# High parts of q and k written straight into the scores' tiles, k's low part beside zeros, and new engine times in the planner

## The chip, the core and the metric

One core of a Trainium2 chip runs the whole program. The metric is device microseconds (us) of one execution. The kernel before took 2547.5 us (median of three runs, 2544.88 to 2548.47).

The names of the profile: PE is TensorE (matmuls; PEld its weight loads), DVE is VectorE, ACT is ScalarE, POOL is GpSimd, SP is SyncE, whose queue issues the DMA transfers. Each engine takes its instructions strictly in the order in which they were written for it, and waits at the first whose inputs or output buffer are not ready.

## The reference, cut to what matters

The program is a two-layer encoder on 512 tokens of 1024 features, in float32. Each layer is:

```
x = x + 0.5 * swiglu_ffn(x, ffn1_norm, w_gate, w_up, w_down)      # 1024 -> 2816 -> 1024
h = rms_norm(x, mix_norm)
aq, ak, av, bq, bk, bv, cq, ck, cv, cg, gates = split(h @ w_in)
y_a = diff_attention(rope(norm(aq)), rope(norm(ak)), av, ...)     # 4 heads x 2 score maps, v 128 wide, rms norm of each head
y_b = chunk_attention(norm(bq), norm(bk), bv, rel_bias)           # 8 heads, 64 wide
y_c = silu(cg) * rms(retention(rope(cq), rope(ck), cv))           # 4 heads, q and k 64 wide, v 128 wide
merged = sum over a, b, c of sigmoid(gate) * (y @ w_branch)
x = x + merged @ w_out
x = x + 0.5 * swiglu_ffn(x, ffn2_norm, ...)
```

In A and B the attention weights are `softmax(q·k * scale + mask or bias)`; in C they are `q·k * decay`. q and k have 64 features per head.

## The kernel before, in words

**Precision.** A float32 product is made of three matmuls: each operand is split into a high part in the `fp32r` type (one ACT copy) and a low part (what is left, one DVE subtraction), and the program multiplies hi·hi, hi·lo and lo·hi. For the scores, where q and k have only 64 features and TensorE contracts over 128 rows, the three products fit into two matmuls: q's tile holds hi in one half of its 128 rows and lo in the other; k's first tile holds hi in both halves, k's second tile holds lo in both halves (`scores`, `dots`).

**The main stream.** Weights come in 212 pieces of 128x1024 per layer as `wr` (one SP transfer of 512 KB each, L195), ACT writes `wh`, DVE `wl`, and 5088 matmuls of 128x512 per layer use them. These are called main matmuls below and counted from the start of a layer: ffn1 to 1584; the projections of A's q, k, v and B's q, k, v, 96 each, to 2160; **branch A**: its eight gate projections (`proj` of `xn`) to 2352, four projections for C's output gate (`c_gates`) to 2448, then 96 products of A's result with its branch weights to 2544; C's q, k and v to 2736; **branch B**: eight gate projections to 2928, products to 3024; **branch C**: gate projections to 3216, products to 3312; `w_out` to 3504; ffn2 to 5088. This order is fixed in `mixer` and `branch`.

**The side programs.** Everything else of the mixers is written as Python generators, and a planner mixes them into the main stream while the program is written. `prep` normalises q or k of A or B (`rsqrt` on 128x32 numbers, eleven or twelve small DVE operations, then one DVE operation for each of four tiles `z`), transposes them on PE in four head pairs (four transposes each), splits each bank of PSUM into `qh` and `ql`, and lets `stack` and `twice` copy the halves into the scores' tiles `qk` by SP transfers (L661). `c_prep` does the same for C, whose halves come rotated out of the projection, by transfers of 32 rows (L1012). `a_head`, `b_head` and `c_head` make scores, softmax, transposes of the weights and products with v. In A and C a head ends in `settle_head`: the result `yu` and its square `sq` are copied from PSUM, `yh` and `yl` are the split of the square, and two matmuls against `ones` total the square over features; the totals go into `ss`. `finish` then takes two heads at a time: `rsqrt_wide` on 128x512 numbers (v, r, then three rounds of three DVE operations, and for C one more), two small SP transfers `rh<-r` per head (L763), one or two DVE operations on `yu`, and its split into `yh` and `yl` for the branch products.

**The planner.** `Model` keeps an estimated time for each engine and adds an estimated cost to it for every instruction that is written (`note`, L89); `sent` (L85) estimates when a transfer has landed. After every main matmul `tick` (L249) may let one side program take one step, if the Model says that its inputs are ready, that no backlog is above 5 us, and that the pace allows it (`due`). `branch` (L1029) needs a finished list `ys`: where its flag is not up when its gate projections are written, it calls `drain(flag)` (L1042), and for branch C `drain()` (L1044) in any case: the side programs are then written out with no main matmul between them. All the Model's numbers act on the order alone; the chip never sees them.

**Buffers.** All 128x512 tiles come from one ring of 72 buffers (`big`), in the order in which they are asked for; eight PSUM banks likewise.

Of the kernel before, what the change touches and what calls it, by code (L numbers as in the profile page):

```python
# [51 lines left out]
class Model:  # L52
# [3 lines left out]
    def __init__(self):  # L56
        self.t = dict(pe=0.0, dve=0.0, act=0.0, pool=0.0)
        self.wrote = {}
        self.read = {}
        self.slots = [0.0] * 8  # L60
        self.owner = {}

# [21 lines left out]

    def sent(self, ap, wait=2500):  # L85

        self.wrote[self.key(ap)] = max(self.t.values()) + wait, "pe"

    def note(self, eng, op, named):  # L89
# [5 lines left out]
        if "dma" in op:  # L95
            for a in outs:
                self.wrote[self.key(a)] = max(self.t[eng], self.t["pe"]) + 2500, eng
            return
        if eng == "pe":
            if op == "transpose":  # L100
                d = 109
            elif named["rhs"].dtype == F32R:
                d = n / 2.37 if n >= 256 else 213
            else:
                d = max(n, 64) * 1.7
# [17 lines left out]
def then(*aps):  # L123

    return aps, False, 0
# [7 lines left out]
def room(*aps):  # L133

    return aps, True, Kernel.MARGIN


class Kernel:
# [467 lines left out]
    def prep(self, z, ms, out, flag, tabs=None, final=None, gain=None):  # L606
# [4 lines left out]
        for b in range(NB):  # L611
# [12 lines left out]
            yield then()  # L624
        parts = None
        for pr in range(4):
            yield room(*z)
            bank = self.bank()
            for b in range(NB):
                nc.tensor.transpose(bank[:, b * P:(b + 1) * P], z[b][:, pr * P:(pr + 1) * P], self.ident)  # L630
            if pr:
                self.stack(parts, out, flag)
            yield then(bank)
            hi, lo = parts = self.big(F32R, "qh"), self.big(F32R, "ql")
            g = 1.0 if gain is None else gain
            nc.scalar.activation(out=hi, in_=bank, func=AF.Copy, scale=g)
            yield then(hi)
# [4 lines left out]
            self.free(bank)  # L642
        yield then(lo)
        self.stack(parts, out, flag)
# [12 lines left out]
    def twice(self, a, b, own, other):  # L657

        t = self.big(F32R, "qk")
        for o, x in ((own, a), (other, b)):  # L660
            self.nc.sync.dma_start(out=t[o].bitcast(F32), in_=x.bitcast(F32))  # L661
        self.model.sent(t)
        return t

# [110 lines left out]
    def a_head(self, h, st):  # L775
# [11 lines left out]

        yield room(*(st[s][2 * h + c][0] for s in "qk" for c in range(2)))
        for i in range(NB + 1):
# [24 lines left out]
    def b_head(self, h, st):  # L814
        nc = self.nc
        tb = self.table()
        es = self.weights()
        yield room(*(st[s][h][0] for s in "qk"))
        for i in range(NB):
# [29 lines left out]
    def c_head(self, h, st):  # L849
# [3 lines left out]
        pt = self.turned()  # L853
        yield room(q[0], k[0], k[1])
        for j in range(NB):
# [141 lines left out]
    def c_prep(self, halves, out, s):  # L997


        parts = []  # L1000
        for y in halves:
            parts.append((yield from self.split_side(y)))
        yield then(parts[1][1])
        for h in range(4):
            hi, lo = ([p[i][32 * h:32 * h + 32] for p in parts] for i in range(2))
            a, b = h % 2 * 64, 64 - h % 2 * 64
            both = []
            for one, two in ((hi, hi), (lo, lo)) if s == "k" else ((hi, lo),):
                t = self.big(F32R, "qk")
                for at, pieces in ((a, one), (b, two)):  # L1010
                    for i, x in enumerate(pieces):
                        self.nc.sync.dma_start(out=t[at + 32 * i:at + 32 * i + 32].bitcast(F32), in_=x.bitcast(F32))  # L1012
                self.model.sent(t)
                both.append(t)
            out.append((both[0], both[-1]))
            self.flags.add(f"{s}C{h}")
# [196 lines left out]
```

## Time and profile before

| | |
|---|---|
| median of 3 runs | 2547.5 us (2544.88 to 2548.47) |
| the profiled execution's own time | 2552.16 us |
| its span | 2550.4 us |
| mean granted TensorE clock | 0.996 |
| PE busy | 2517.2 us (99%) |
| DVE, ACT, POOL busy | 1375.7 (54%), 919.8 (36%), 138.3 us (5%) |
| SP transfers into scores' tiles | 96 `qk<-qh`, 96 `qk<-ql`, 48 `qk<-yh`, 48 `qk<-yl` |

The span runs from the first instruction to the last; the execution's own time is 1.8 us longer. A layer's projections and branches lie between about 380 and 850 us in the first layer and between about 1650 and 2120 us in the second. All compute instructions have line L48 (they pass through the planner's wrapper), so they are told apart by their tiles: `bank<-xh,wh` is a projection, `bank<-ident,z` a transpose in `prep`, `bank<-yh,ones` a total, `bank<-ident,e` a transpose of softmax weights `e`.

### The profile page before, as it was taken

To read this page: it belongs to the slowest core of one execution; us is meant where nothing else is said; L and a number is where in the kernel's file an instruction comes from. 1 tells how busy PE (TensorE), PEld (TensorE's weight loads), DVE (VectorE), ACT (ScalarE), POOL (GpSimd) and SP (SyncE) were. 2 spreads that over 40 slices of the span, in tenths; PEclk is the share of its full clock that TensorE was granted. 3 is DMA by queue.
4 is the path that set the end of the run, shared out by engine and by line. 5 is a ranking of instruction groups with operands and counts; after the bars stand their busy time and mean duration, and the time that the engine had idled before them with its cause. 6 is when DMAs were issued, how large, how long until landed. Compare 5 with 4: busy or idle time off the path is not lost.

```text
span 2550.4 us, 28931 instructions
## 1 busy us (share of the span) xinstructions
PE 2517.2 (99%) x11226; PEld 2054.4 (81%) x11226; DVE 1375.7 (54%) x2180; ACT 919.8 (36%) x1397; POOL 138.3 (5%) x104
## 2 busy tenths in 40 slices
PE   9999999999999999999999999999999999999999
PEld 7888887887878888888888888878878788888887
DVE  6334338776758653433353433477767576543332
ACT  4333224553443433332233332245534433333321
POOL 0000101000102100000000001010001021000000
PEclk9999999999999999999999999999999999999999
DMA  5333344527433433333333333344274324333332
GB/s 167 92 99 91 118 130 123 134 83 190 115 105 83 140 99 99 92 99 94 96 92 98 91 97 114 120 133 123 85 196 113 106 76 146 99 94 99 91 111 71
DMA packets 96617, 280.91 MB, mean 110 GB/s; under 512 B 13536, under 2 KB 14944, under 8 KB 96480
## 3 DMA queue, kind: packets, MB, share of 16 engines
q1 hardware_dynamic: 95760, 278.45, 38.2%
q8 instruction: 88, 1.44, 0.2%
q10 hardware_dynamic: 720, 0.62, 0.1%
q14 instruction: 49, 0.40, 0.0%
HBM read 237.08 MB, written 6.29 MB: 95 GB/s over the span
## 4 chain that ended last, share of the span: by engine, by line
PE 93%; DVE 3%; SPq 2%; DMA 1%; issue 0%; ACT 0%; DVEq 0%
PE bank L48 93%; SPq L661 1%; SPq L1012 1%; DVE wl L48 1%; DMA qk<-ql 1%; DVE e L48 0%; DMA x<-in_xt 0%; DVE n L48 0%; DVE g L48 0%; DVE z L48 0%; DVE pt L48 0%; DVE r L48 0%; DMA qk<-yh 0%; DVE ql L48 0%; ACT wh L48 0%
## 5 line engine op out<-in xcount | busy, mean ns | idle before, releaser
L48 DVE TENSOR_TENSOR wl<-wr,wh 128x1024 fp32r<-128x1024 f32 x422 | 530.8, 1259 | 705.7 <-ACT wh L48 703.6
L48 PE MATMUL bank<-xh,wh 128*128 128x512 f32 x1920 | 758.8, 395 | 0.0
L48 PE MATMUL bank<-xl,wh 128*128 128x512 f32 x1920 | 757.6, 395 | 0.1
L48 PE MATMUL bank<-xh,wl 128*128 128x512 f32 x1920 | 756.3, 394 | 0.0
L48 ACT ACTIVATE wh<-wr 128x1024 fp32r<-128x1024 f32 x422 | 445.4, 1056 | 775.2 <-PE bank L48 671.2
L48 PEld LDWEIGHTS bank<-xh,wh 128*128 128x128 f32 x1920 | 361.9, 188 | 78.2 <-ACT xh L48 1.2
L48 PEld LDWEIGHTS bank<-xl,wh 128*128 128x128 f32 x1920 | 362.0, 189 | 77.9 <-DVE xl L48 1.7
L48 PEld LDWEIGHTS bank<-xh,wl 128*128 128x128 f32 x1920 | 361.9, 188 | 77.7
L48 PE MATMUL bank<-ph,wh 128*128 128x512 f32 x704 | 276.6, 393 | 0.0
L48 PE MATMUL bank<-pl,wh 128*128 128x512 f32 x704 | 276.6, 393 | 0.0
L48 PE MATMUL bank<-ph,wl 128*128 128x512 f32 x704 | 276.6, 393 | 0.0
L48 PE MATMUL bank<-wl,xh 128*128 128x512 f32 x448 | 179.2, 400 | 0.0
L48 PE MATMUL bank<-wh,xh 128*128 128x512 f32 x448 | 178.8, 399 | 0.0
L48 PE MATMUL bank<-wh,xl 128*128 128x512 f32 x448 | 178.2, 398 | 0.0
L48 PEld LDWEIGHTS bank<-ph,wh 128*128 128x128 f32 x704 | 132.4, 188 | 29.6
L48 PEld LDWEIGHTS bank<-ph,wl 128*128 128x128 f32 x704 | 132.4, 188 | 29.4
L48 PEld LDWEIGHTS bank<-pl,wh 128*128 128x128 f32 x704 | 132.4, 188 | 29.4
L48 ACT ACTIVATE e<-e,m 128x128 f32<-128x128 f32 (+3 forms) x128 | 71.4, 558 | 118.8 <-DVE m L48 105.0
L48 ACT ACTIVATE t<-t 128x512 f32<-128x512 f32 x88 | 55.6, 632 | 162.5 <-DVE t L48 162.5
L48 POOL TENSOR_TENSOR acc<-acc,sq 128x512 f32<-128x512 f32 x30 | 39.4, 1314 | 1112.1 <-PE bank L48 567.7
L48 PEld LDWEIGHTS bank<-wh,xh 128*128 128x128 f32 x448 | 84.3, 188 | 17.0
L48 PEld LDWEIGHTS bank<-wl,xh 128*128 128x128 f32 x448 | 84.4, 188 | 16.8
(145 smaller groups left out, 2486.1 us busy)
## 6 DMA issues: line engine op xcount, KB each, us to landing
wr<-in_w SPq DMA_DIRECT2D x422, 512.0 KB, 3.6
qk<-qh SPq DMA_DIRECT2D x96, 128.0 KB, 4.2
qk<-ql SPq DMA_DIRECT2D x96, 128.0 KB, 3.8
xd<-x SPq DMA_DIRECT2D x16, 256.0 KB, 2.7
tb<-in_tbias SPq DMA_DIRECT2D x16, 256.0 KB, 3.3
rh<-r SPq DMA_DIRECT2D x32, 128.0 KB, 4.9
x<-xd SPq DMA_DIRECT2D x16, 256.0 KB, 5.6
qk<-yh SPq DMA_DIRECT2D x48, 64.0 KB, 2.0
```

The costliest lines, as they stand in the source:

```text
L48: return call(*args, **kw)
L661: self.nc.sync.dma_start(out=t[o].bitcast(F32), in_=x.bitcast(F32))
L1012: self.nc.sync.dma_start(out=t[at + 32 * i:at + 32 * i + 32].bitcast(F32), in_=x.bitcast(F32))
```

## The change: what it does

1. `split_pair` replaces the split in `prep`. ACT writes hi of each head of a pair (64x512) straight into its half of that head's scores' tile `qk`; DVE writes lo of each head apart. For q, lo goes to a tile `ql`, and one transfer per head brings it into the other half of `qk`. For k, one transfer per head copies hi into the other half, and lo goes into the right half of a tile `kl` of its own, whose other half POOL sets to zero. `twice` is gone.
2. `c_prep` sets k's low part beside zeros likewise: six transfers of 32 rows for each head of k in place of eight.
3. k's second tile thus holds (lo; 0) in place of (lo; lo): the product lo·lo is left out of every score. The number of matmuls is the same.
4. `Model`: new formulas for the cost of an instruction on each engine (all higher), a term by which DVE operations with two operands in SBUF and POOL operations exclude each other, 4.5 us in place of 2.5 us for a transfer to land.
5. The heads' first step waits (in the Model) for all tiles of q and k, not for the first of each.

```diff
-    def sent(self, ap, wait=2500):
+    def sent(self, ap, wait=4500):
...
+        in_sbuf = sum(x.space != bass.MemoryType.PSUM for x in ins)
         if eng == "pe":
...
-                d = n / 2.37 if n >= 256 else 213
+                d = max(n, 256) * 0.452
...
         elif eng == "dve":
-            plain = not any(a.space == bass.MemoryType.PSUM for a in ins + outs)
-            d = 68 + n / (1.92 if op == "tensor_scalar" and plain else 0.96)
+            plain = in_sbuf == len(ins) and not any(a.space == bass.MemoryType.PSUM for a in outs)
+            d = 220 + n * 0.53 if op == "tensor_scalar" and plain else 130 + n * 1.1
             d += 60 * by_row
+            d += 85 * ("accum_out" in aps)
         elif eng == "act":
-            d = (50 if aps["in_"].space == bass.MemoryType.PSUM else 93) + n * 0.834 + 93 * by_row
+            d = (165 if aps["in_"].space == bass.MemoryType.PSUM else 207) + n * 0.834 + 93 * by_row
+            d += 187 * ("accum_out" in aps)
         else:
-            d = 100 + n * 2.2
+            d = 170 + n * 2.4
         at = max([self.t[eng]] + [self.ready(a, eng) for a in ins])
+        if eng == "dve" and in_sbuf > 1 or eng == "pool":
+            at = max([at] + [end for start, end in self.port if start <= at])
+            self.port = self.port[-7:] + [(at, at + d)]
...
+    HALF = (slice(0, 64), slice(64, P))
+
+    def split_pair(self, bank, gain, is_q):
+        nc = self.nc
+        his = [self.big(F32R, "qk") for _ in range(2)]
+        los = [self.big(F32R, "ql")] * 2 if is_q else [self.big(F32R, "kl") for _ in range(2)]
+        g = lambda r: 1.0 if gain is None else gain[r]
+        if not is_q:
+            for t, other in zip(los, self.HALF[::-1]):
+                nc.gpsimd.memset(t[other].bitcast(F32), 0.0)
+        for t, r in zip(his, self.HALF):
+            nc.scalar.activation(out=t[r], in_=bank[r], func=AF.Copy, scale=g(r))
+        yield then(*his)
+        for t, lo, r in zip(his, los, self.HALF):
             if gain is None:
-                nc.vector.tensor_tensor(out=lo, in0=bank, in1=hi.bitcast(F32), op=ALU.subtract)
+                nc.vector.tensor_tensor(out=lo[r], in0=bank[r], in1=t[r].bitcast(F32), op=ALU.subtract)
             else:
-                nc.vector.scalar_tensor_tensor(out=lo, in0=bank, scalar=g, in1=hi.bitcast(F32), op0=ALU.mult, op1=ALU.subtract)
...
-    def stack(self, parts, out, flag):
-        hi, lo = parts
-        is_q = flag[0] == "q"
-        half = (slice(0, 64), slice(64, P))
-        for r, other in zip(half, half[::-1]):
-            t = self.twice(hi[r], lo[r] if is_q else hi[r], r, other)
-            out.append((t, t if is_q else self.twice(lo[r], lo[r], r, other)))
+    def stack(self, pair, out, flag):
+        his, is_q, los = pair
+        for t, lo, r, other in zip(his, los, self.HALF, self.HALF[::-1]):
+            self.nc.sync.dma_start(out=t[other].bitcast(F32), in_=(lo if is_q else t)[r].bitcast(F32))
+            self.model.sent(t)
+            out.append((t, t if is_q else lo))
...
-        yield room(*(st[s][2 * h + c][0] for s in "qk" for c in range(2)))
+        yield room(*(t for s in "qk" for c in range(2) for t in st[s][2 * h + c]))
...
-            both = []
-            for one, two in ((hi, hi), (lo, lo)) if s == "k" else ((hi, lo),):
-                t = self.big(F32R, "qk")
-                for at, pieces in ((a, one), (b, two)):
-                    for i, x in enumerate(pieces):
-                        self.nc.sync.dma_start(out=t[at + 32 * i:at + 32 * i + 32].bitcast(F32), in_=x.bitcast(F32))
+            t = self.big(F32R, "qk")
+            moves = [(t, a, hi), (t, b, hi if s == "k" else lo)]
+            if s == "k":
+                low = self.big(F32R, "kl")
+                self.nc.gpsimd.memset(low[b:b + 64].bitcast(F32), 0.0)
+                moves.append((low, a, lo))
+            for to, at, pieces in moves:
+                for i, x in enumerate(pieces):
+                    self.nc.sync.dma_start(out=to[at + 32 * i:at + 32 * i + 32].bitcast(F32), in_=x.bitcast(F32))
```

By the instructions' lists, SP issues 681 transfers in place of 825: those into the scores' tiles of A and B go from 192 to 64, those of C from 96 to 80. ACT has 32 activations more and DVE 32 operations more (64x512 in place of half as many of 128x512), POOL has 40 settings to zero of 64x512. PE has as many instructions as before. The planner's new numbers move many instructions; three places follow.

**PE where branch A's products begin (main matmul 2448 of layer 1).** `bank<-xh,w...` are the gate projections, `z` the tiles of B's q and k in `prep`, `yh,ones` a total, `bank<-yh,wh` the first branch product. Before:

```order
L48 MATMUL bank_4796<-ident,z_3802 128x128
L48 MATMUL bank_4796<-ident,z_3813 128x128
L48 MATMUL bank_4796<-ident,z_3824 128x128
L48 MATMUL bank_4796<-ident,z_3835 128x128
L48 MATMUL bank_4741<-xl_2525,wh_4650 128x512
L48 MATMUL bank_4741<-xh_2524,wl_4651 128x512
L48 MATMUL bank_4827<-yh_3935,wh_4690 128x512
L48 MATMUL bank_4827<-yl_3936,wh_4690 128x512
```

And now (the last projection stands 17 rows above the first of these):

```order
L48 MATMUL bank_4694<-ident,z_3373 128x128
L48 MATMUL bank_4694<-ident,z_3384 128x128
L48 MATMUL bank_4738<-ident,z_3581 128x128
L48 MATMUL bank_4738<-ident,z_3595 128x128
L48 MATMUL bank_4738<-ident,z_3606 128x128
L48 MATMUL bank_4738<-ident,z_3617 128x128
L48 MATMUL bank_4757<-ident,z_3581 128x128
L48 MATMUL bank_4757<-ident,z_3595 128x128
L48 MATMUL bank_4757<-ident,z_3606 128x128
L48 MATMUL bank_4757<-ident,z_3617 128x128
L48 MATMUL bank_4783<-yh_4333,wh_4512 128x512
L48 MATMUL bank_4783<-yl_4334,wh_4512 128x512
```

Before, one group of four transposes stands among the last projections, and a branch product follows the last of them directly. Now 26 rows of side programs stand between the last projection and the first product: 24 transposes (16 of B's q, 8 of B's k) and the two matmuls of the last of A's four totals. The second of these stands 17 rows ahead of the first product; before, the last total stood 177 rows ahead of it.

**DVE at the same place.** `cg` and `cs` are C's output gate (`bank` of a projection, times `rb`), `y_` the last step of the small `rsqrt` and `z` the tiles scaled with it, `yu` in `finish`, `kl` and `ql` the low parts. Before:

```order
L48 TENSOR_TENSOR z_3835<-z_3835,y_4630 128x512
L48 TENSOR_TENSOR cg_4685<-bank_4653,rb_2602 128x512
L48 SCALAR_TENSOR_TENSOR cs_4686<-cs_4686,cg_4685 128x512
L48 TENSOR_TENSOR yl_4615<-yu_4291,yh_4614 128x512
L48 TENSOR_TENSOR wl_4691<-wr_4575,wh_4690 128x1024
L48 SCALAR_TENSOR_TENSOR yu_4363<-yu_4363,sub_1966,rh_4556 128x512
L48 TENSOR_TENSOR cg_4733<-bank_4693,rb_2602 128x512
```

And now:

```order
L48 SCALAR_TENSOR_TENSOR n_4718<-y_4717,v_4716 128x32
L48 TENSOR_TENSOR n_4718<-n_4718,y_4717 128x32
L48 SCALAR_TENSOR_TENSOR y_4717<-n_4718,y_4717 128x32
L48 TENSOR_TENSOR z_3581<-z_3581,y_4717 128x512
L48 TENSOR_TENSOR z_3595<-z_3595,y_4717 128x512
L48 TENSOR_TENSOR z_3606<-z_3606,y_4717 128x512
L48 TENSOR_TENSOR z_3617<-z_3617,y_4717 128x512
L48 SCALAR_TENSOR_TENSOR yu_4443<-yu_4443,sub_1966,rh_4708 128x512
L48 TENSOR_TENSOR yl_4736<-yu_4443,yh_4735 128x512
L48 SCALAR_TENSOR_TENSOR yu_4620<-yu_4620,sub_1966,rh_4711 128x512
L48 SCALAR_TENSOR_TENSOR kl_4745<-bank_4738,cols_74,qk_4743 64x512
L48 SCALAR_TENSOR_TENSOR kl_4746<-bank_4738,cols_74,qk_4744 64x512
```

Before, the scaling of the four `z` of B's q stands between evacuations of projections still to come, and that of B's k comes after the branch has begun. Now both are written before the branch's first product, the last four `z` (B's k) behind the last evacuation of a projection, behind the wide rsqrt of `finish`, six `ql` and the small rsqrt.

**DVE where branch C's products begin (main matmul 3216 of layer 1).** `r_` is the last operation of the wide rsqrt in C's `finish` for heads 3 and 4, `g<-bank,rb` the evacuation of a gate projection, `yu`, `yl` the rest of `finish`. Before:

```order
L48 TENSOR_SCALAR r_6791<-r_6791 128x512
L48 TENSOR_TENSOR g_6817<-bank_6770,rb_2602 128x512
L48 TENSOR_TENSOR g_6848<-bank_6823,rb_2602 128x512
L48 TENSOR_TENSOR wl_6821<-wr_6684,wh_6820 128x1024
L48 TENSOR_TENSOR wl_6852<-wr_6746,wh_6851 128x1024
L48 TENSOR_TENSOR g_6891<-bank_6857,rb_2602 128x512
L48 SCALAR_TENSOR_TENSOR yu_6617<-yu_6617,cols_74,rh_6863 128x512
L48 TENSOR_TENSOR yu_6617<-yu_6617,cs_4734 128x512
L48 TENSOR_TENSOR wl_6895<-wr_6787,wh_6894 128x1024
L48 TENSOR_TENSOR yl_6910<-yu_6617,yh_6909 128x512
L48 SCALAR_TENSOR_TENSOR yu_6731<-yu_6731,cols_74,rh_6866 128x512
L48 TENSOR_TENSOR yu_6731<-yu_6731,cs_4820 128x512
```

And now:

```order
L48 TENSOR_SCALAR r_6853<-r_6853 128x512
L48 TENSOR_TENSOR g_6875<-bank_6827,rb_2603 128x512
L48 TENSOR_TENSOR g_6906<-bank_6881,rb_2603 128x512
L48 SCALAR_TENSOR_TENSOR yu_6619<-yu_6619,cols_74,rh_6909 128x512
L48 TENSOR_TENSOR yu_6619<-yu_6619,cs_4583 128x512
L48 TENSOR_TENSOR yl_6918<-yu_6619,yh_6917 128x512
L48 SCALAR_TENSOR_TENSOR yu_6807<-yu_6807,cols_74,rh_6912 128x512
L48 TENSOR_TENSOR yu_6807<-yu_6807,cs_4630 128x512
L48 TENSOR_TENSOR yl_6924<-yu_6807,yh_6923 128x512
L48 TENSOR_TENSOR wl_6879<-wr_6761,wh_6878 128x1024
```

Before, five evacuations of gate projections are still to come when the wide rsqrt ends (three of them in these rows). Now two are, both of projections that PE has done by then, and the next weights to be split (`wl`) stand behind the whole of `finish`. On PE, the last of C's four totals stood 120 rows ahead of the branch's first product before, and stands 37 rows ahead of it now, 36 of them main matmuls.

More of the change, by code (lines that the diff above doesn't have):

```diff
@@ L60, in __init__ @@
         self.slots = [0.0] * 8
+        self.port = []
         self.owner = {}
@@ L102, in note @@
             elif named["rhs"].dtype == F32R:
-                d = n / 2.37 if n >= 256 else 213
+                d = max(n, 256) * 0.452
             else:
-                d = max(n, 64) * 1.7
+                d = max(n, 64) * 1.72
         elif eng == "dve":
-            plain = not any(a.space == bass.MemoryType.PSUM for a in ins + outs)
-            d = 68 + n / (1.92 if op == "tensor_scalar" and plain else 0.96)
+            plain = in_sbuf == len(ins) and not any(a.space == bass.MemoryType.PSUM for a in outs)
+            d = 220 + n * 0.53 if op == "tensor_scalar" and plain else 130 + n * 1.1
             d += 60 * by_row
+            d += 85 * ("accum_out" in aps)
         elif eng == "act":
-            d = (50 if aps["in_"].space == bass.MemoryType.PSUM else 93) + n * 0.834 + 93 * by_row
+            d = (165 if aps["in_"].space == bass.MemoryType.PSUM else 207) + n * 0.834 + 93 * by_row
+            d += 187 * ("accum_out" in aps)
         else:
-            d = 100 + n * 2.2
+            d = 170 + n * 2.4
         at = max([self.t[eng]] + [self.ready(a, eng) for a in ins])
+        if eng == "dve" and in_sbuf > 1 or eng == "pool":
+            at = max([at] + [end for start, end in self.port if start <= at])
+            self.port = self.port[-7:] + [(at, at + d)]
         self.t[eng] = at + d
@@ L624, in prep @@
             yield then()
-        parts = None
+        pair = None
         for pr in range(4):
@@ L631, in prep @@
             if pr:
-                self.stack(parts, out, flag)
+                self.stack(pair, out, flag)
             yield then(bank)
[L634 to L637, printed above, removed]
+            pair = yield from self.split_pair(bank, gain, flag[0] == "q")
+        yield then(*pair[2])
+        self.stack(pair, out, flag)
@@ L638, in prep @@
             if gain is None:
-                nc.vector.tensor_tensor(out=lo, in0=bank, in1=hi.bitcast(F32), op=ALU.subtract)
+                nc.vector.tensor_tensor(out=lo[r], in0=bank[r], in1=t[r].bitcast(F32), op=ALU.subtract)
             else:
-                nc.vector.scalar_tensor_tensor(out=lo, in0=bank, scalar=g, in1=hi.bitcast(F32), op0=ALU.mult, op1=ALU.subtract)
-            self.free(bank)
-        yield then(lo)
-        self.stack(parts, out, flag)
-    def stack(self, parts, out, flag):
-        hi, lo = parts
-        is_q = flag[0] == "q"
-        half = (slice(0, 64), slice(64, P))
-        for r, other in zip(half, half[::-1]):
-            t = self.twice(hi[r], lo[r] if is_q else hi[r], r, other)
-            out.append((t, t if is_q else self.twice(lo[r], lo[r], r, other)))
-        self.flags.add(f"{flag}{len(out) // 2 - 1}")
@@ L657, in twice @@
-    def twice(self, a, b, own, other):
-        t = self.big(F32R, "qk")
[L660 to L663, printed above, removed]
+                nc.vector.scalar_tensor_tensor(out=lo[r], in0=bank[r], scalar=g(r), in1=t[r].bitcast(F32), op0=ALU.mult, op1=ALU.subtract)
+        self.free(bank)
+        return his, is_q, los
+    def stack(self, pair, out, flag):
[4 more added lines that the diff above has]
+            out.append((t, t if is_q else lo))
+        self.flags.add(f"{flag}{len(out) // 2 - 1}")
@@ L817, in b_head @@
         es = self.weights()
-        yield room(*(st[s][h][0] for s in "qk"))
+        yield room(*(t for s in "qk" for t in st[s][h]))
         for i in range(NB):
@@ L853, in c_head @@
         pt = self.turned()
-        yield room(q[0], k[0], k[1])
+        yield room(*q, *k)
         for j in range(NB):
@@ L1006, in c_prep @@
             a, b = h % 2 * 64, 64 - h % 2 * 64
-            both = []
-            for one, two in ((hi, hi), (lo, lo)) if s == "k" else ((hi, lo),):
-                t = self.big(F32R, "qk")
-                for at, pieces in ((a, one), (b, two)):
-                    for i, x in enumerate(pieces):
[L1012 to L1015, printed above, removed]
+            t = self.big(F32R, "qk")
[7 more added lines that the diff above has]
+                    self.nc.sync.dma_start(out=to[at + 32 * i:at + 32 * i + 32].bitcast(F32), in_=x.bitcast(F32))
+                self.model.sent(to)
+            out.append((t, low if s == "k" else t))
             self.flags.add(f"{s}C{h}")
```

## The prediction

> **What bounds the kernel now.** I began with the page's totals: PE is busy nearly throughout.
>
> ```profile
> span 2550.4 us, 28931 instructions
> PE 2517.2 (99%) x11226; PEld 2054.4 (81%) x11226; DVE 1375.7 (54%) x2180; ACT 919.8 (36%) x1397; POOL 138.3 (5%) x104
> ```
>
> So the change can win only what PE loses, some 33 us of idle time and what the clock costs. The view of PE's waits says on whom (total, times, longest, in us; `yl` at the end is a branch's or a total's input):
>
> ```profile
> PE bank L48 <- DVE e L48: 17.4, 6, 5.2
> PE bank L48 <- DMA qk<-ql: 3.5, 6, 0.8
> PE bank L48 <- DVE z L48: 3.4, 2, 1.7
> ...
> PE bank L48 <- DVE yl L48: 0.6, 2, 0.3
> ```
>
> Then the busy time by stretches (columns: length; busy time and count of PE, PEld, DVE, ACT, POOL; granted clock of PE; DMA share and GB/s), for the places where these waits lie and for clean stretches:
>
> ```profile
> 410.00:420.00 10.00, 8.28 (x41) 6.54 (x40) 8.67 (x11) 5.88 (x10) 4.00 (x3) 1.00 0.34 107
> 605.00:637.00 32.00, 25.64 (x115) 19.89 (x114) 17.90 (x47) 12.06 (x25) 0.00 (x0) 0.95 0.84 212
> 704.00:716.00 12.00, 6.90 (x31) 5.41 (x30) 4.91 (x10) 3.69 (x7) 0.00 (x0) 0.86 0.59 163
> 1682.00:1692.00 10.00, 8.28 (x40) 6.58 (x39) 8.67 (x12) 6.02 (x10) 4.14 (x3) 1.00 0.34 102
> 1876.00:1910.00 34.00, 28.37 (x120) 22.14 (x119) 19.61 (x50) 12.94 (x27) 0.00 (x0) 0.90 0.80 201
> 1976.00:1990.00 14.00, 8.84 (x39) 7.13 (x38) 5.97 (x14) 4.70 (x9) 0.00 (x0) 0.76 0.59 174
> 1000.00:1032.00 32.00, 32.00 (x141) 26.28 (x140) 12.82 (x15) 9.71 (x12) 0.00 (x0) 1.00 0.34 99
> 1000.00:1100.00 100.00, 100.00 (x438) 82.08 (x437) 40.65 (x46) 30.46 (x36) 0.00 (x0) 1.00 0.32 95
> 1300.00:1400.00 100.00, 100.00 (x430) 81.03 (x429) 39.89 (x45) 30.49 (x36) 0.00 (x0) 1.00 0.32 93
> ```
>
> A clean stretch does 141 matmuls in 32 us: 0.227 us each. A stretch loses its length less PE's busy time, and its length times the missing clock: 1.7 us at 410, 6.4 + 1.6 = 8.0 at 605, 5.1 + 1.7 = 6.8 at 704; in layer 2 again 1.7, 5.6 + 3.4 = 9.0 and 5.2 + 3.4 = 8.5. That is nearly all the idle time. The two clean rows of 100 us differ by 8 matmuls, 1.8 us: some ffn stretches run at a slower pace, which I come back to as an uncertainty.
>
> The stall at 605 is that of B's k. The timelines of SP, DVE and PE show it, and that of C's k at 704:
>
> ```profile
> 614.97 1.10 SPq L661 DMA_DIRECT2D qk<-qh  x2
> 624.25 1.19 SPq L661 DMA_DIRECT2D qk<-ql  x2
> 631.89 0.46 PE L48 MATMUL bank<-ident,e 128*128 128x128 f32 x1 [2.61 <-DVE e L48]
> ...
> L1012 SPq DMA_DIRECT2D qk<-yh x16: 513/588/591, 690.8 to 707.8; - x16
> 709.23 0.75 DVE L48 SCALAR_TENSOR_TENSOR vl<-bank,rt,vh 128x512 fp32r<-128x512 f32 x1 [7.31 <-DMA qk<-yh]
> 710.63 0.47 PE L48 MATMUL bank<-ident,e 128*128 128x128 f32 x1 [5.10 <-DVE e L48]
> ```
>
> One transfer takes SP 0.6 us, and B's prep needs 64 of them per layer. At 704, `vl` comes behind C's 32 transfers: its ring buffer is still being read by one of them; `e` is queued behind `vl` on DVE, and PE behind `e`.
>
> **What the change removes.** In A and B 128 transfers fewer, 64 per layer, and 8 fewer per layer in C. SP's train for B's k, 32 transfers before, becomes 8. I take the stalls at 410, 605, 1682 and 1876 as gone: 1.7 + 8.0 + 1.7 + 9.0 = **20.4 us**. (At 410 the late work is DVE's `z` in A's prep; the new order gives it more distance.) The bounds are 16 (half of B's stall in each layer stays as softmax work) and 28 (all the idle time but C's stall and the program's ends). The additions of part 1 of the change are small: 32 ACT activations of 0.6 us, 32 DVE operations of 0.74 us and 40 memsets over two layers lie on engines that are busy 36, 54 and 5%; they cost PE nothing but in the chains below, where I count them.
>
> **What the new order adds at branch A.** Here the lists of instructions decide. PE's last total of A now comes behind the last gate projection, and between it and the first product stand transposes of `z_3617`, which DVE scales behind the wide rsqrt of that very total. No main matmul is written in between, so PE can't start the chain earlier, and has almost nothing to do while it runs. Its links, by the groups with equal shapes kept together, and two rows of DVE's timeline for the spacing in a wide rsqrt:
>
> ```profile
> L48 DVE TENSOR_TENSOR cg<-bank,rb 128x512 f32<-128x512 f32 x8 | 5.5, 687 | 2.7 <-PE bank L48 2.5
> L48 ACT ACTIVATE cs<-cg 128x512 f32<-128x512 f32 x8 | 5.1, 632 | 20.3 <-DVE cg L48 20.3
> L48 ACT ACTIVATE yh<-sq 128x512 fp32r<-128x512 f32 x16 | 10.1, 634 | 0.0
> L48 DVE TENSOR_TENSOR yl<-sq,yh 128x512 fp32r<-128x512 f32 x16 | 11.0, 688 | 3.6 <-ACT yh L48 3.4
> L48 ACT ACTIVATE ss<-bank 64x512 f32<-64x512 f32 x16 | 9.5, 595 | 14.0 <-PE bank L48 14.0
> L48 DVE TENSOR_SCALAR v<-ss 128x512 f32<-128x512 f32 x8 | 3.4, 421 | 2.5 <-ACT ss L48 2.5
> L48 DVE TENSOR_SCALAR r<-v 128x512 int32<-128x512 int32 x8 | 3.4, 428 | 0.3
> L48 DVE SCALAR_TENSOR_TENSOR ql<-bank,cols,qh 128x512 fp32r<-128x512 f32 x16 | 11.9, 743 | 0.0
> L48 DVE SCALAR_TENSOR_TENSOR n<-y,v 128x32 f32<-128x32 f32 x24 | 4.6, 192 | 0.8
> L48 DVE TENSOR_TENSOR z<-z,y 128x512 f32<-128x512 f32 x32 | 23.3, 747 | 0.7
> ...
> 786.22 0.69 DVE L48 TENSOR_TENSOR n<-n,r 128x512 f32<-128x512 f32 x1
> 791.30 0.69 DVE L48 SCALAR_TENSOR_TENSOR r<-n,r 128x512 f32<-128x512 f32 x1
> ...
> 418.84 0.60 PE L48 MATMUL bank<-ident,z 128*128 128x128 f32 x4
> 419.52 0.39 PE L48 MATMUL bank<-wh,xl 128*128 128x512 f32 x1
> ```
>
> The seven steps from 786.22 to 791.30 give 0.726 us each. ACT takes `yh` behind `cs`, that is behind the evacuation of the last projection. From the end of that projection: 0.69 + 0.63 + 0.63 until `yh`, about 2.2 us until `ss` is written (`yl`, the total, and two 64x512 activations ahead of `ss` at 0.6); then v 0.42, r 0.43, nine steps 6.5, six `ql` 6 x 0.74 = 4.5, the small rsqrt 11 x 0.19 = 2.1, four `z` 3.0, and 0.8 for the transposes and first use: 22.0 us. PE's own work in it is 24 transposes (four in 0.45 us by the timeline: 2.7) and the total 0.46: 3.2. That leaves 18.8 us idle. Heads 3 and 4 then still need `yu`, `yh`, `yl` on DVE, between B's `kl`: about 2 us beyond what the first six or nine products hide. And the clock comes back late: 1.7 us, by the row at 704, where 5.1 us of pause cost 1.7. Sum **22.5 us per layer**. The lower bound is the part on DVE that nothing can shorten, v to the last `z`, 16.9 - 3.2 = 13.7; the upper 27, if `yl` and the two halves of `qk` interleave badly and the clock costs 3.4 as in layer 2.
>
> The row at 704 agrees with the Trainium skill, "TensorE: Matmul & The Clock Gate", section "What's actually happening" (half rate after an idle window of some 3.4 us, full rate after a busy one). The stretch at 605 fits less: its clock fell to 0.95 with no pause above 2.61 us, but with transposes between the pauses, which the same page, "Part 4: PE-mode transpose", says do not count as busy in the same way. By the first rule alone the next place costs no clock, by the second 1.7 us per layer; the sum is made from the rows either way.
>
> **At branch B** nine PE steps of B's last head and C's first (transposes of `e`, products, scores) are written without main matmuls between. Each waits for its ACT or DVE step: some 13 DVE operations of 0.4 to 0.7 us, about 9 us, against about 5 us of PE's own work. I take 4 idle and 1 of clock, **5 us per layer**, bounds 2 and 8.
>
> **At branch C** the last total has 36 main matmuls of cover, 8.2 us, and the first six products need only heads 1 and 2: 1.4 more. Before, the 120 rows hid it (27 us; no wait on `yl` above 0.3). The chain: the total 0.46, `ss` 0.6, the rsqrt with its last step 7.8, an SP issue 0.6, the landing, and `yu` twice and `yh`, 2.06:
>
> ```profile
> rh<-r SPq DMA_DIRECT2D x32, 128.0 KB, 4.9
> L48 DVE SCALAR_TENSOR_TENSOR yu<-yu,cols,rh 128x512 f32<-128x512 f32 x8 | 6.0, 744 | 7.2 <-DMA rh<-r 7.2
> ```
>
> 16.4 in all, so 16.4 - 8.2 - 1.4 = 6.8 idle, then `yl` 0.7, the last head 2.0 and the clock 1.7: **11.2 us per layer**, bounds 6 and 14.
>
> **C's transfers.** k needs 24 in place of 32, which takes 5 us off the train. But in the new order the buffer of a `pt` that DVE needs for the heads at that time comes from the ring in the place of one that the 21st transfer reads: 21 x 0.6 plus 2 to land is 15 us after the train's start, where DVE is there after about 5 and PE has about 3 of other work. 7 idle and 1.7 of clock against 6.8 and 8.5 before: **+1 us per layer**; bounds -7.6 (gone) and +3.
>
> **Sum.** 2 x (22.5 + 5 + 11.2 + 1) - 20.4 = 79.4 - 20.4 = +59.0 us on the profiled execution's 2552.16, so 2611; its own time lies 4.7 above the median of the runs, so **2606 us** against 2547.5.
>
> **Rivals.** (a) *The waits are half as long*: C's stall vanishes with its train, A's is at its lower bound, B's 2, C's 8: 2 x (13.7 + 2 + 8 - 7.6) - 20.4 = +12, 2560; a mixture with some of it 2585. For it: 8 transfers fewer, and DVE is busy only half the time. Against: the chain at A is strictly serial, and its parts come from rows. (b) *Faster*: at A's branch the rest of `finish` and of the prep is mostly run before PE is through with the projections, so that the drain finds little to do. It decides from under 20.4 / 2 = 10.2 us per layer for the four places together; with 5 per layer it gives 2547.5 - 20.4 + 10 = 2537. For it: before's drains cost PE nothing (`yl` 0.3), where the totals were far ahead. Against: here the total is behind the last projection on PE itself, and from it to the last `z` DVE alone needs 16.9 us. (c) *The pace of ffn*: by the rows at 1000 and 1300 a stretch of 400 us may gain or lose 7 us for no reason in the change. It widens the range; alone it changes no sign. (d) *The transfers are not saved*: the lists exclude it, 681 against 825.
>
> **How the numbers follow.** My forecast, four new waits that cost about three to five times what is won, has 0.78; (a) with its mixture (2560 to 2585) 0.15; (b) 0.06; 0.01 for the rest. Within the forecast the unknown costs give about 2585 to 2632. The range takes in the upper part of (a): 2566 to 2632. A measurement here tells 0.2%, 5 us, from no change. Slower by over that: the forecast and nearly all of (a), 0.91; within it 0.03; faster 0.06.
>
> **What would show it.** In the profile after, PE should idle about 19 us in each layer ahead of branch A's first product (which stood at 605.9 us before in layer 1), waiting for DVE's `z`, with the granted clock at half after it; 7 to 10 us before branch C's products behind `yu` and `rh<-r`; and at C's scores a DVE wait of some 10 us on the transfers of `c_prep`. The stretch behind that product should hold no PE wait above 1 us on `e`. If PE's longest wait is under 8 us, the reading of the lists is wrong; if the waits are there and the time still falls, PE was losing more before than its idle time shows.

## The result

The changed kernel takes 2606.3 us (median of four runs, 2605.1 to 2611.7) against 2548.0 us: a ratio of 1.0235, 95% interval 1.0217 to 1.0253. The profiled execution takes 2607.37 us, 55.2 more than that of before. One of the ten runs of the first experiment below, at a granted clock of 0.56, took 4180.47 us and is left out of its numbers.

The page's totals and the view of PE's waits (total, times, longest, in us) after the change:

```profile
span 2605.5 us, 28848 instructions
PE 2529.6 (97%) x11226; PEld 2062.0 (79%) x11226; DVE 1404.5 (54%) x2212; ACT 943.8 (36%) x1429; POOL 157.4 (6%) x144
...
PE bank L48 <- DVE z L48: 38.6, 4, 16.4
PE bank L48 <- DVE pt L48: 16.6, 8, 7.7
PE bank L48 <- ACT yh L48: 12.1, 6, 4.1
```

The 17.4 us of waits on `e` and the 4.9 us on transfers into `qk` are gone. In their place PE waits for three things: `z` (16.4 us at branch A in each layer), `pt` (at C's transfers), and `yh` (at branch C). The stages of layer 1, cut at the first projection, at branch A's first product, at branch B's first gate projection, at branch C's first product and at `w_out`, show where the time went (columns as in the prediction: stretch and length; busy time and count of PE, PEld, DVE, ACT, POOL; granted clock; DMA share and GB/s). Before:

```profile
371.00:606.00 235.00, 232.77 (x1089) 190.30 (x1088) 178.39 (x384) 113.67 (x209) 10.52 (x8) 1.00 0.48 125
606.00:701.00 95.00, 88.64 (x424) 71.47 (x423) 65.98 (x152) 42.80 (x94) 10.10 (x6) 0.98 0.56 146
701.00:844.00 143.00, 137.61 (x643) 113.24 (x642) 96.78 (x160) 59.34 (x104) 15.25 (x8) 0.99 0.35 99
844.00:866.00 22.00, 22.00 (x97) 17.83 (x96) 18.26 (x21) 8.91 (x14) 8.76 (x6) 1.00 0.59 194
```

And after:

```profile
372.00:628.40 256.40, 235.25 (x1083) 191.48 (x1082) 188.53 (x393) 120.74 (x218) 18.89 (x23) 0.96 0.35 95
628.40:722.50 94.10, 86.41 (x410) 70.73 (x409) 63.61 (x136) 43.96 (x88) 13.17 (x11) 0.95 0.44 123
722.50:862.70 140.20, 139.22 (x662) 114.76 (x662) 98.61 (x177) 61.14 (x113) 13.41 (x8) 1.00 0.29 85
862.70:894.00 31.30, 26.36 (x97) 20.00 (x96) 22.42 (x28) 11.57 (x16) 8.71 (x6) 0.84 0.47 152
```

Up to branch A's first product the layer has become 21.4 us longer (3.0 of them at the stall at 410, as the account below works out), in branch C's products 9.3 us. The two stages between are 3.7 us shorter: there the stalls on B's transfers went, and one at C's grew. In all +27.0 us; the same cuts in layer 2 (371 to 866 there is 1643 to 2138.5) give +26.5. Together 53.5 of the span's 55.1. The ffn stages have not changed.

### The profile page after: what moved, and what is told of

It reads as the page before. It is cut to its first block, busy times and chain, and to the rows that moved or that the text cites. A ratio compares the mean times of both kernels' runs of the same rounds, so it can differ in the third digit from the quotient of the medians.

```text
span 2605.5 us, 28848 instructions
## 1 busy us (share of the span) xinstructions
PE 2529.6 (97%) x11226; PEld 2062.0 (79%) x11226; DVE 1404.5 (54%) x2212; ACT 943.8 (36%) x1429; POOL 157.4 (6%) x144
## 4 chain that ended last, share of the span: by engine, by line
PE 94%; DVE 3%; DMA 1%; SPq 1%; ACT 1%; issue 1%; DVEq 0%; ACTq 0%
PE bank L48 94%; DVE n L48 1%; DVE z L48 1%; SPq L1028 0%; DVE ql L48 0%; DVE r L48 0%; DMA x<-in_xt 0%; DVE pt L48 0%; DVE yu L48 0%; DVE w L48 0%; DMA rh<-r 0%; DMA qk<-yh 0%; ACT yh L48 0%; ACT wh L48 0%; DVE d L48 0%
```

## The experiments

**The two halves of the change apart.** One kernel has the new movement, with the wider wait of the heads' first step, and the planner's old engine times (the new terms for accumulation and for the exclusion of DVE and POOL, in the lines left out, are gone too):

```diff
-    def sent(self, ap, wait=4500):
+    def sent(self, ap, wait=2500):
...
-                d = max(n, 256) * 0.452
+                d = n / 2.37 if n >= 256 else 213
...
-            d = 220 + n * 0.53 if op == "tensor_scalar" and plain else 130 + n * 1.1
+            d = 68 + n / (1.92 if op == "tensor_scalar" and plain else 0.96)
...
-            d = (165 if aps["in_"].space == bass.MemoryType.PSUM else 207) + n * 0.834 + 93 * by_row
+            d = (50 if aps["in_"].space == bass.MemoryType.PSUM else 93) + n * 0.834 + 93 * by_row
...
-            d = 170 + n * 2.4
+            d = 100 + n * 2.2
```

> The changed movement of q and k (split_pair, stack, c_prep, the wider room) with the planner's engine times of before. In its list of instructions A's last total stands 154 main matmuls (35 us at 0.227) ahead of branch A's first product, C's 94 ahead of branch C's. Theory: the loss is the order that the new engine times give, and the movement alone is a small gain: no wait of PE on DVE z above 4 us at branch A, 2525 to 2550 us. Rival: the movement itself (halves of 64x512, two activations and two subtractions for one, memsets) makes the chains longer: 2575 to 2606 us.

Measured: a ratio to before of 1.0003, 0.9983 to 1.0022 (2554.17 us against 2552.52 in the same session). No loss, but the small gain that the theory forecast isn't there either: the time lies just above its range. PE's longest wait on `z` is 1.7 us; the stalls on B's transfers are mostly gone (2.8 us on `e` in place of 17.4) and others have come, the largest on `pt` at C's transfers:

```profile
PE bank L48 <- DVE pt L48: 12.1, 4, 5.4
PE bank L48 <- ACT yh L48: 4.9, 2, 2.4
PE bank L48 <- DVE z L48: 3.4, 2, 1.7
```

The other kernel has the old movement and the new times (the same edit the other way round, in the kernel before).

> The movement of before with the planner's new engine times. A's last total stands 19 main matmuls ahead of branch A's first product, with 20 instructions of side programs between the last projection and the product; C's 46 ahead. Theory: slower than before by the order alone, and without the shorter trains of transfers: 2590 to 2625 us, with a PE wait of 10 us or more at branch A. Rival (the movement costs the time): at most 2560 us.

Measured: 2618.9 us, ratio 1.0267 (1.0238 to 1.0295). The new times alone cost at least as much as the whole change (the two intervals, 1.0238 to 1.0295 and 1.0217 to 1.0253, overlap).

```profile
PE bank L48 <- DVE z L48: 27.6, 4, 10.9
PE bank L48 <- DVE m L48: 11.7, 5, 3.6
```

So the loss lies in the order that the planner writes, and not in how q and k are moved.

**Which of the planner's times.** The changed kernel with DVE's formula put back:

```diff
-            plain = in_sbuf == len(ins) and not any(a.space == bass.MemoryType.PSUM for a in outs)
-            d = 220 + n * 0.53 if op == "tensor_scalar" and plain else 130 + n * 1.1
+            plain = not any(a.space == bass.MemoryType.PSUM for a in ins + outs)
+            d = 68 + n / (1.92 if op == "tensor_scalar" and plain else 0.96)
...
-            d += 85 * ("accum_out" in aps)
```

> The changed kernel with only the planner's formula for DVE's times put back (68 + n/0.96, half for tensor_scalar, nothing for accumulation). A's last total now stands 122 main matmuls ahead of branch A's first product. Theory: DVE's times decide how late the planner lets the heads' steps be, and so the whole loss: 2525 to 2550 us, below the kernel before if the shorter trains are worth something. Rival: all the new times together delay (ACT's, PE's, the 4.5 us for a transfer): 2580 to 2606 us.

Measured: 2530.2 us, ratio 0.992 (0.9902 to 0.9938): 0.8% below the kernel before. PE's waits on `z` and `pt` don't occur any more; what is left is a transfer of B's and 4.3 us on `yh`:

```profile
PE bank L48 <- DMA qk<-qk: 8.4, 2, 4.5
```

And the opposite, the old times with only DVE's formula new:

```diff
-            plain = not any(a.space == bass.MemoryType.PSUM for a in ins + outs)
-            d = 68 + n / (1.92 if op == "tensor_scalar" and plain else 0.96)
+            plain = in_sbuf == len(ins) and not any(a.space == bass.MemoryType.PSUM for a in outs)
+            d = 220 + n * 0.53 if op == "tensor_scalar" and plain else 130 + n * 1.1
...
+            d += 85 * ("accum_out" in aps)
```

> The new movement with the planner's times of before, and only DVE's formula new (130 + 1.1 n and its terms). A's last total stands 0 main matmuls ahead of branch A's first product, C's 51. Theory: DVE's formula alone brings the wait at branch A back, 16 us on z per layer with the clock behind it, and about half of the rest: 2575 to 2600 us. Rival (the loss needs several of the new times together): at most 2560 us.

Measured: 2575.4 us, ratio 1.0097 (1.0068 to 1.0125). The wait at branch A is back:

```profile
PE bank L48 <- DVE z L48: 35.7, 4, 15.9
PE bank L48 <- ACT yh L48: 9.5, 6, 2.3
```

DVE's formula alone brings some two fifths of the loss, most of it at branch A; the half of the rest that the theory counted on did not come, and the time lies at the lower edge of its range. The waits on `pt` (16.6 us in the changed kernel) aren't there: these need the other times too. The effects don't add up: by the ratios, DVE's old formula takes 80 us off the changed kernel (1.0235 to 0.992), and the new one adds 24 to the old times with the new movement (1.0003 to 1.0097).

**The formula as a dose.** The measured time of a 128x512 operation is 686 ns; the new formula says 693, the old 601. Two kernels give it other values, all else as changed:

```diff
-            d = 220 + n * 0.53 if op == "tensor_scalar" and plain else 130 + n * 1.1
+            d = 220 + n * 0.53 if op == "tensor_scalar" and plain else 0 + n * 0.7
```

> The changed kernel with the planner's time for a DVE operation set far too low: 0.7 n in place of 130 + 1.1 n ns (358 in place of 693 for 128x512; the trace has 686). A's last total now stands 262 main matmuls ahead of branch A's first product. Theory: the price is two-sided. No drain waits above 3 us at the branches, but DVE is late at many steps of the heads and PE waits there in many small pieces: 2560 to 2610 us. Rival (the earlier the side work, the better): below 2530 us, the time with the old formula.

and, with `30 + n * 1.0` in the same place:

> The same formula at 30 + 1.0 n ns (542 for 128x512, a fifth below the measured 686), the other DVE terms as in the changed kernel. A's last total stands 154 main matmuls ahead of the branch. Theory: near the optimum between late drains and small waits, as with the old formula: 2515 to 2540 us. Rival (the new formula for DVE is right, and only its accumulation and tensor_scalar terms did the harm): 2570 to 2606 us.

| planner's time for 128x512 on DVE | main matmuls between A's last total and branch A | median us (ratio, interval) |
|---|---|---|
| 358 ns | 262 | 2594.3 (1.0178, 1.0161 to 1.0194) |
| 542 ns | 154 | 2513.3 (0.9859, 0.9843 to 0.9875) |
| 601 ns (old formula, with its old terms for other operations) | 122 | 2530.2 (0.992, 0.9902 to 0.9938) |
| 693 ns (the change) | 0 | 2606.3 (1.0235, 1.0217 to 1.0253) |

At 358 ns the waits are many and small, as expected: PE finds steps of the side programs written before DVE is through with their inputs.

```profile
PE bank L48 <- DVE z L48: 23.2, 12, 3.6
PE bank L48 <- DMA qk<-yh: 9.3, 2, 4.7
PE bank L48 <- DVE pt L48: 6.5, 8, 1.4
```

At 542 ns nearly nothing is left to wait for, and this is the fastest kernel of the study, 1.4% below the kernel before:

```profile
PE bank L48 <- DVE e L48: 3.6, 4, 0.9
...
PE bank L48 <- DMA qk<-qk: 1.3, 1, 1.3
```

Of these four the number that is nearest to the truth gives the slowest kernel, and one that is a fifth too low the fastest.

**Is it a smooth optimum?** With `20 + n * 1.0`, 532 in place of 542 ns:

> As the run with 30 + 1.0 n, but 20 + 1.0 n ns (532 in place of 542 for 128x512, 2%). A's last total stands 141 main matmuls ahead in place of 154, C's 97 in place of 121. Theory A: time is a smooth function of the planner's number, with its best near here: 2510 to 2525 us. Theory B: each list falls into or out of single collisions (a buffer that a transfer still reads, a transfer that is late), so that 2% of a number can cost a per cent: above 2535 us, with one new wait of 5 us or more per layer.

Measured: 2562.7 us, ratio 1.0041 (1.0025 to 1.0057): 2% of one number cost 46 us by the ratios. The new waits are collisions with C's transfers, as theory B has it. PE's waits, then a row each of DVE's and PE's timeline:

```profile
PE bank L48 <- DVE m L48: 26.2, 4, 7.6
...
694.24 0.42 DVE L48 CUSTOM_DVE_ANT_0 e<-bank,tb 128x256 f32<-128x256 f32 x1 [10.74 <-DMA qk<-yh]
694.82 1.19 PE L48 MATMUL bank<-pt,vv 128*128 128x512 f32 x2 [7.12 <-DVE m L48]
```

DVE stands 10.7 us at an `e` whose wait ends with a transfer of C's prep, which no softmax of B needs as data. So the table above shows which side of the truth is dangerous at branch A, and not a curve on which one could choose a value beforehand.

**What the movement is worth in a good order.** The kernel before with all the new times, but DVE at `30 + n * 1.0`; this line is the one that differs from the run with the new times alone:

```diff
-            d = 68 + n / (1.92 if op == "tensor_scalar" and plain else 0.96)
+            d = 220 + n * 0.53 if op == "tensor_scalar" and plain else 30 + n * 1.0
```

> The movement of before with the new engine times except DVE's at 30 + 1.0 n ns, the formula that gave 2513 us with the new movement. A's last total stands 158 main matmuls ahead, C's 98. Theory: the movement is worth something once the order is good, since B's 64 and C's transfers per layer come back as waits: 2525 to 2545 us. Rival (the movement is worth nothing, as with the planner's old times): 2510 to 2520 us.

Measured: ratio 1.0003 (0.9989 to 1.0018), 2549.8 us, a little above what either theory gave, where the new movement has 2513.3. With these times, then, the kernel with the new movement is some 36 us faster; with the old times it was no faster. That the movement itself is worth these 36 us is not shown: the two orders differ too (C's last total stands 98 main matmuls ahead of its branch, and 121 with the new movement), and in the run above 2% of a number moved the time by 46 us. The waits are those of before, on B's transfers and on `vl` behind C's:

```profile
PE bank L48 <- DVE vl L48: 10.5, 2, 5.3
...
PE bank L48 <- DMA qk<-ql: 4.5, 8, 1.0
```

**The chain at branch A by itself.** The changed kernel without two of the three rounds of the wide rsqrt in A's finish (`rounds` is 1 there and 3 elsewhere; the planner still counts the operations left out, so the rest keeps its order):

```diff
-        for _ in range(3):
+        for i in range(3):
             yield then()
+            if i >= rounds:
+                note = self.model.note
+                note("dve", "scalar_tensor_tensor", dict(out=t, in0=y, scalar=-0.5, in1=val))
+                note("dve", "tensor_tensor", dict(out=t, in0=t, in1=y))
+                note("dve", "scalar_tensor_tensor", dict(out=y, in0=t, scalar=1.5, in1=y))
+                continue
```

> The changed kernel with two of the three rounds of the wide rsqrt in A's finish left out (six DVE operations of 0.726 us in each of its two uses per layer), while the planner still counts them, so that the order of all the rest stays. It leaves out part of the refinement of A's norm. Theory: the chain at branch A is serial on DVE from the total to the last z, so PE's wait on z there falls from 16.4 by 4.4 us, and the time by 8.7 us for two layers: about 2597 us. Rival (PE waits there for something beside that chain: the halves of q on ACT, the transposes, a buffer): less than 3 us, 2603 to 2606.

Measured: 2600.9 us, ratio 1.0202 (1.0178 to 1.0226); by the ratios of the two kernels 8 us less than the changed one, though the intervals overlap, and the time lies between the theory's and the rival's. The trace is clearer: six operations of 0.726 us are left out of the chain, and the wait falls from 16.4 to 12.0 us, by these 4.4.

```profile
PE bank L48 <- DVE z L48: 29.9, 4, 12.0
```

**The buffer at C's transfers.** One buffer more in the ring, the same order of instructions:

```diff
-    RING = 72
+    RING = 73
```

> The changed kernel with 73 in place of 72 buffers in the ring; the order of all instructions on each engine is the same, only which tile follows which in a buffer differs. Theory: PE's waits on DVE pt (16.6 us, longest 7.7) come from a pt tile that takes a buffer which the transfers of c_prep still read; with another pairing they shrink to under 10 us: 2592 to 2603 us. Rival: pt waits for what the transfers bring, so nothing changes: 2603 to 2609 us. Branch A's 16.4 us on z stays in both.

Measured: 2605.4 us, ratio 1.0215 (1.0177 to 1.0253): no difference that the time could show; it lies in the rival's range. The waits decide for the theory. PE's, then one of ACT's:

```profile
PE bank L48 <- ACT pt L48: 9.6, 2, 5.1
PE bank L48 <- DVE pt L48: 1.8, 4, 0.6
...
ACT pt L48 <- DMA qk<-yh: 14.3, 2, 7.4
```

DVE's `pt` no longer waits for a transfer, so that wait was the buffer's and not the data's, which were the same. But now the next `pt`, ACT's, gets a buffer that a transfer still reads. The wait has moved by one tile and PE's 7.7 us became 5.1.

**The remaining waits of the old formula.** Old DVE formula, no exclusion of DVE and POOL in the planner, 6.0 us for a transfer:

```diff
-    def sent(self, ap, wait=4500):
+    def sent(self, ap, wait=6000):
...
-        if eng == "dve" and in_sbuf > 1 or eng == "pool":
-            at = max([at] + [end for start, end in self.port if start <= at])
-            self.port = self.port[-7:] + [(at, at + d)]
```

> Old DVE formula, no exclusion of DVE and POOL in the planner, and 6.0 us for a transfer to land; the other new times and the new movement stay. A's last total stands 164 main matmuls ahead, C's 138. With the old DVE formula alone PE still waited 4.5 us for a transfer qk<-qk in each layer and 3 to 6 us at branch C. Theory: with later scores and an earlier C both go: 2510 to 2526 us. Rival (what those waits give up comes back as others): 2526 to 2540 us.

Measured: 2519.1 us, ratio 0.9888 (0.9866 to 0.9911). Neither the transfer nor branch C is waited for any more; the longest wait on the side programs is 2.3 us, on `pt`.

## Why the prediction was right, step by step

The time (2606 forecast, 2606.3 measured) and the mechanism were right. Part of the closeness is luck: the terms are off by up to 4 us per layer in both directions, and the sum was made for the profiled executions, where it gave 59.0 us and 55.2 were measured. The forecast then took off 4.7 us, by which the profiled execution of before lay above its median; the one after lies only 1.1 above.

**Branch A: 22.5 us forecast, 20 to 21 measured.** The chain ran as the list was read. DVE's and PE's timelines, and two stretches around the end of the wait:

```profile
605.03 0.69 DVE L48 TENSOR_TENSOR cg<-bank,rb 128x512 f32<-128x512 f32 x1 [1.38 <-PE bank L48]
609.83 0.43 DVE L48 TENSOR_SCALAR v<-ss 128x512 f32<-128x512 f32 x1
617.69 4.66 DVE L48 SCALAR_TENSOR_TENSOR ql<-bank,cols,qk 64x512 fp32r<-64x512 f32 x6
624.84 2.50 DVE L48 TENSOR_TENSOR z<-z,y 128x512 f32<-128x512 f32 x4
...
625.59 3.13 PE L48 MATMUL bank<-ident,z 128*128 128x128 f32 x8 [16.39 <-DVE z L48]
...
600.00:625.50 25.50, 7.74 (x43) 6.04 (x41) 21.16 (x39) 9.76 (x15) 3.11 (x6) 0.71 0.32 75
625.50:635.00 9.50, 9.03 (x35) 6.83 (x36) 8.56 (x13) 6.69 (x10) 1.04 (x2) 0.69 0.22 48
```

From the evacuation of the last projection to the end of the last `z` it takes 605.03 to 627.3, 22.3 us; the sum was 22.0 to the first use. PE idles 17.8 + 0.5 us in the two stretches (18.8 forecast), and the clock costs at most 0.31 x 9.5 = 2.9 after the pause (1.7 forecast); that is an upper bound, since DVE's last `z`, to 627.3, would have held the transposes back at any clock. The stage gives the lower figure: 21.4 less the 3.0 at 410, and some 1.5 of slow products behind the cut. The 2 us for heads 3 and 4 did not appear: the products wait for nothing behind the transposes. The slow clock lasted through the eight transposes, from 625.59, and then for some 3.1 us of products more:

```profile
628.00:632.00 4.00, 4.00 (x16) 3.24 (x15) 3.14 (x6) 3.79 (x6) 0.52 (x1) 0.57 0.30 66
632.00:636.00 4.00, 4.00 (x22) 3.26 (x21) 3.89 (x6) 3.87 (x6) 0.00 (x0) 1.00 0.00 0
```

That agrees with the Trainium skill, "TensorE: Matmul & The Clock Gate": a busy window of about 3.4 us restores the clock ("What's actually happening"). The same page says that transposes don't count towards it in the same way ("Part 4: PE-mode transpose"); this trace doesn't show that they are why the slow clock lasted here. At branch C of the same layer no transposes come first, and the products ran without a pause from 871.08 to 877.1, 6.0 us, before the full clock was back:

```profile
872.00:876.00 4.00, 4.00 (x10) 3.13 (x11) 2.62 (x3) 0.00 (x0) 1.24 (x1) 0.50 0.64 223
877.38 0.40 PE L48 MATMUL bank<-yh,wl 128*128 128x512 f32 x1
```

So the clock's price of one pause doesn't carry over to another; the last section says what these traces show of it.

**What goes: 20.4 forecast.** For B's stalls right, and rather low: no PE wait on `e` is left, and by the stages cut above the time between branch A's first product and C's has fallen although C's stall there grew. But the step "at 410 the late work is DVE's `z` in A's prep; the new order gives it more distance" was wrong: the wait grew, from 1.7 us to

```profile
423.39 0.47 PE L48 MATMUL bank<-ident,z 128*128 128x128 f32 x1 [2.93 <-DVE z L48]
415.00:435.00 20.00, 17.07 (x77) 13.62 (x76) 16.78 (x20) 10.56 (x16) 9.60 (x12) 0.91 0.41 109
```

and 0.09 x 20 = 1.8 us of clock with it: 4.7 in place of 1.7 in each layer, 6 us in all where -3.4 were in the sum. The new memsets are not the cause: the run with the old movement, which has none, waits 2.93 us at this place as well, and the run with the new movement and the old times 1.72. The rows show what holds DVE up:

```profile
417.88 2.94 DVE L48 TENSOR_TENSOR w<-z,tab 128x256 f32<-128x256 f32 x2
414.41 6.13 POOL L48 TENSOR_TENSOR u<-z,tab 128x512 f32<-128x512 f32 x4 [16.46 <-ACT z L48]
```

POOL's four `u` now stand back to back, and DVE's two `w` beside them take 2.94 us, where two take 0.75 without POOL (at 410.25). (A slip beside this: the prediction counts 64 transfers per layer for B's prep. By the lists' 192 for A and B in two layers it is 48; nothing in the sum rests on it.)

**Branch B: 5 forecast, 1 measured.** Mis-sized: the ACT and DVE steps overlap with PE's far better than a sum of thirteen DVE operations, and the clock stays at 1.00.

```profile
760.00:790.00 30.00, 29.02 (x147) 23.49 (x146) 21.04 (x45) 16.43 (x35) 0.00 (x0) 1.00 0.28 82
```

**Branch C: 11.2 forecast, 9.3 measured** (31.3 less 22.0 us, the stage in layer 1). DVE's and PE's timelines:

```profile
862.72 0.43 DVE L48 TENSOR_SCALAR r<-r 128x512 f32<-128x512 f32 x1
866.11 0.75 DVE L48 SCALAR_TENSOR_TENSOR yu<-yu,cols,rh 128x512 f32<-128x512 f32 x1 [1.77 <-DMA rh<-r]
868.30 0.79 PE L48 MATMUL bank<-yh,wh 128*128 128x512 f32 x1 [4.11 <-ACT yh L48]
```

The chain is the one named, `r`, `rh`, `yu`, `yh`, but from the end of `r` to `yu` it takes 3.0 us where an issue of 0.6 and a landing of 4.9 were put in (the page has 3.4 us for `rh<-r` after and had 4.9 before; that fewer transfers on the queue are why was not tried). PE idles 31.3 - 26.36 = 4.9 us in the stage, where 9.5 were in the sum and 7 to 10 among the signs to look for; the other 4.4 are the slow clock, where 1.7 were. Two misses cancel here.

**C's transfers: +1 forecast as the mean of both layers; +2.6 to +4.2 measured in layer 1, +0.3 to +2.1 in layer 2.** The mechanism was as told. DVE's and PE's timelines:

```profile
712.59 0.56 DVE L48 TENSOR_TENSOR pt<-bank,pt 128x384 fp32r<-128x384 f32 x1 [8.15 <-DMA qk<-yh]
713.21 0.90 PE L48 MATMUL bank<-pt,vv 128*64 128x384 f32 x2 [7.69 <-DVE pt L48]
690.00:720.00 30.00, 22.31 (x107) 17.97 (x106) 13.21 (x29) 11.29 (x23) 2.19 (x4) 0.89 0.51 137
```

PE idles 7.7 us (7 forecast); the clock's share of 0.11 x 30 = 3.3 is an upper bound, since part of it falls into the pause, and 1.7 as before a lower one: 9.4 to 11.0 against 6.8. In layer 2 the same sum (25 - 17.91 of idle time at 1995 to 2020, 1.7 to 0.14 x 25 of clock) gives 8.8 to 10.6 against 8.5. Too small in layer 1 was the pause, by 0.7, and the clock's price. The run with 73 buffers showed that the buffer is the cause.

**The terms together.** In layer 1 they give 20 to 21 + 1 + 9.3 + 2.6 to 4.2, and 3.0 more at 410, less B's 8.0: 27.9 to 30.5 us, where the stages have 27.0 and the forecast 30.0. So B's stall was worth somewhat more than 8.0, or the bounds of the clock's share are too high; the traces don't tell which.

The rival that the waits are half as long fell with PE's 16.4 us at branch A and 7.7 at C's transfers, the rival of a gain with the total on PE behind the last projection. The two paces of ffn were there but cancelled: one of the four ffn stages is at the slower pace in both profiles.

## What to carry to other kernels

Where a planner fixes the order of instructions from estimated engine times, judge its change by the order it writes and not by how true its times are: look for the last link of a chain that has moved behind the last piece of covering work, and add up the chain behind it from rows of the profile. Times that are truer can be worse, since an estimate that is a little low costs small waits where a late tail costs all of its length; and single collisions, a buffer that a transfer still reads, make the time jump for 2% of a number, so try several values on the chip. What a saving is worth can hide behind the order: with the same transfers saved the kernel was no faster with one set of planner's times and 36 us faster with another.

## What the runs showed of the hardware that was not expected

The granted clock falls and returns on a grid. In all thirteen profiles the trace's record of it holds 0.50 for whole multiples of 3.41 us (from 3.41 to 23.89 us; a last stretch runs into the program's end). In the changed kernel these are 3.41 us at 410, 20.48 at branch A and 6.83 at C's transfers, and at branch C 10.24 in layer 1 and 6.83 in layer 2, where PE's wait was the same 4.1. Each time the clock came back at the end of the first piece of 3.41 us that PE had filled but for 0.2 us at most. So each piece in which PE works at half pace costs up to half of its length, 1.7 us, and how many a pause brings depends on where in the grid it falls.

TensorE streams the same ffn matmuls at two paces with the granted clock at 1.00 in both: 431 or 439 matmuls in 100 us. In the changed kernel, and in the fastest one, at the same place of the span:

```profile
1300.00:1400.00 100.00, 100.00 (x431) 81.12 (x430) 47.03 (x56) 30.05 (x36) 0.00 (x0) 1.00 0.32 93
...
1300.00:1400.00 100.00, 100.00 (x439) 82.04 (x438) 40.60 (x46) 30.83 (x38) 0.00 (x0) 1.00 0.32 98
```

In these two, ffn1 of layer 2 is 7 us apart (369.9 and 363.0 us). Before and after the change the slower pace sets in within that stage, at the norm's total (`bank<-yh,ones`, at 1282.2 and 1310.5): 0.229 us per matmul ahead of it, 0.233 behind it. In nine of the thirteen profiles of this study, before and after among them, one of the four ffn stages is at the slower pace; in those of the three fastest kernels and of the one at 358 ns none is. Runs of the kernel before lie between 2541 and 2560 us, 19 us apart; that the pace is a part of this was not shown, and what chooses the pace stays open.
